# Seven products of quarters for eight in the first product of two squared-ReLU stages

## The chip, the cores and the metric

The kernel runs on one core of a Trainium2 chip, as one launch. The metric is the device time of that core in microseconds (us), the median of the runs. Engines are named as in the profile: PE (TensorE matmul), PEld (its weight loads), DVE (the vector engine), ACT (the scalar engine), POOL (GpSimd), SP (the engine that issues most DMAs).

## What is computed

Two transformer blocks for 16 meta tokens and 512 tokens of width 1024, all in float32. The second block has two layers, each an attention followed by a squared-ReLU stage, and these two stages are what the change touches:

```python
def sq_relu_mlp(x, w1, w2):
    h = jax.nn.relu(x @ w1)
    return (h * h) @ w2
...
        hn = rms_norm(h, attn_norm[i])
        if i < N_A:
            h = h + dsa_attention(hn, a_w_in[i], ...)
        else:
            ...
            h = h + fox_attention(hn, b_w_q[j], ...)
        h = h + sq_relu_mlp(rms_norm(h, mlp_norm[i]), mlp_w1[i], mlp_w2[i])
```

`w1` is 1024 x 4096 and `w2` 4096 x 1024. The first stage works on T = 528 tokens, the second on the S = 512 that are asked for.

## The kernel before

Activations are kept transposed: 8 tiles of 128 partitions (features) by the tokens. A float32 product is made of three float32r matmuls: each factor is split into a high part (a rounded copy, by ACT) and a low part (the difference, by DVE), and high x high, high x low and low x high are summed in PSUM. For weights this is `weight_parts` (`wh` at L82 by ACT, `wl` at L83 by DVE), for activations `split` (L106 and L107, or L109 and L110 where a factor per partition goes in).

`products` (matmul at L99) makes a block of 128 outputs: 8 tiles of depth x 3 matmuls for each stretch of tokens. In the first squared-ReLU stage a block takes two stretches of 264 tokens, in the second, where `k.whole` is set, one of 512. So a pair of blocks costs 2 x 2 x 24 = 96 matmuls of 264 columns there, and 2 x 24 = 48 of 512 columns here.

`mlp` (L1390) runs a stage. It first has the attention before it add its heads' outputs to the residual `h` (`before()`, which is `Dsa.out` at L1004 for the first stage and `Fox.out` at L1464 for the second): for each of 8 output tiles j a block of products from the attention's output (`bigh`, `bigl`), added to `h` by DVE (L857). `operand` (L893) then makes the stage's input from `h` times the norm's weights, split into `xh` and `xl` (L109, L110), one tile at a time, and sums the squares (ACT at L159 and L162, POOL at L163). `token_rsqrt` (L900) sums them over the partitions with 5 matmuls (L171), takes 1/sqrt by twelve small DVE operations (L131 to L138) and brings the result to all partitions with 5 transposes (L182) and two ACT copies (L907). These factors enter when the products are taken out of PSUM (L1407), so the products don't wait for them.

The 32 blocks of `w1` come in two chunks of 16. Each block is taken out by DVE (L1407, ReLU and norm), squared by ACT (L1410) and split (L106, L107). After a chunk `down` (L934, matmul at L948) multiplies its 16 tiles by `w2`, 8 output tiles at a time of two blocks of weights each, and DVE adds the result to `h` (L857). PSUM has 6 banks for products and 2 for the rest.

The order of the instructions on each engine is fixed when the program is built: a scheduler with a model of the engines' times puts them in order (the program's order gives the priority), and each engine then works its list strictly in order, waiting on semaphores. SP issues the weights' loads in its own list; a buffer of weights (`wr`, three of 512 KB) is free again when DVE has split it.

Of the kernel before, what the change touches and what calls it, by code (L numbers as in the profile page):

```python
# [46 lines left out]
class K:  # L47
    """The kernel's context: engines, pools and the pieces that recur."""

    def __init__(self, tc):  # L50
# [4 lines left out]

    def psum(self, **banks):
        """A pool of PSUM banks, so many a tag, for a phase."""
        self.banks = banks
# [14 lines left out]
    def weights(self, wdram, kt=8):  # L73
        """A block of kt tiles of weights, split into two float32r parts that sum to it exactly."""
# [11 lines left out]
    def dense(self, wdram, xh, xl, evac, kt=8, lo=0, n=T):  # L86
        """One block of 128 outputs for n tokens, a bank of them at a time: evac(products, tokens) takes them over."""
# [60 lines left out]
    def squares(self, tiles, pool=None, lo=0, eng=None):  # L148
        """Sums over the tiles of their squares from token lo on, [128, tokens] with zeros around."""
# [15 lines left out]
    def sumsq(self, acc, chunks):  # L165
        """The sums over the partitions too, as columns of PSUM (a column a chunk of tokens)."""
# [7 lines left out]
    def rows(self, cols, chunks, take, tags=("pa", "pa")):  # L174
        """The transposes of cols(chunk) [tokens, 128], to take(values, tokens)."""
# [44 lines left out]
# -------------------------------------------------------------------- first layer  # L220
# blocks of w_in: a head's q, k, v, then z, sc_b, sc_c, sc_x, gate_a, gate_b
# [9 lines left out]
class Layer1:  # L231
# [13 lines left out]
    def normed(self, out, lo=0):  # L245
        """Takes over the products of the tokens from lo on with their norm."""
# [47 lines left out]
    def gates(self):  # L294
        """Log decays, their running sums by chunks and betas."""
# [7 lines left out]
        with tc.tile_pool(name="l1g", bufs=1) as pg:  # L303
            G = self.G  # rows 0..15 beta, 32..47 decay; no decay where there is no token
# [118 lines left out]
    def sc_out(self, j):  # L423
        """2 sigmoid(gate_b) y_b for 128 features, in place of the gate."""
# [7 lines left out]
    # ---- independent of the recurrence  # L432
# [1422 lines left out]
```

## Time and profile before

| | |
|---|---|
| median of 3 runs | 2609.57 us (2607.39 to 2611.97) |
| span of the profiled execution | 2607.7 us, 1.9 us below that median; no separate time of this execution is listed |
| PE busy | 2523.1 us, 97% of the span |
| DVE, ACT, POOL busy | 1535.0, 1072.2, 438.4 us |
| mean granted TensorE clock | 0.979 of full speed |
| first squared-ReLU stage | about 1522 to 1895 us after the span's start |
| second squared-ReLU stage | about 2244 to 2604 us |

Matmuls overlap in the pipe, so PE's busy share says little about how close matmuls follow each other; the number of matmuls that start in a stretch of a window says it. The rows of a timeline give start, duration, engine, source line, what is written and read, and in brackets how long the engine had been idle and who released it.

### The profile page before, as it was taken

Reading aid. Unit: us, or ns where it says so; the run is one execution under the profiler, and the core shown is the slowest. Engines: PE = TensorE matmul, PEld = TensorE weight load, DVE = VectorE, ACT = ScalarE, POOL = GpSimd, SP = SyncE. Lnnn points to the kernel's source line nnn. Section 1 sums busy time; section 2 is a strip of 40 time slices with the busy share of each in tenths; the row PEclk is TensorE's granted clock in tenths of the full one; section 3 lists DMA queues with packets and bytes.
Section 4 is the critical chain, followed back from the end, with each engine's and each line's share of the span. In section 5 each row is a group of like instructions: output and inputs, shape, how many; then the busy total and the mean of one; then the engine's idle time right before and its main releaser. Section 6 shows DMA issues by size and latency. Waiting matters only on the chain.

```text
span 2607.7 us, 45619 instructions
## 1 busy us (share of the span) xinstructions
PE 2523.1 (97%) x18012; PEld 2315.5 (89%) x18012; DVE 1535.0 (59%) x3288; ACT 1072.2 (41%) x2191; POOL 438.4 (17%) x599
## 2 busy tenths in 40 slices
PE   8899999999999999999879999999999999999999
PEld 8889999999899888888868999999999988788887
DVE  7878788766554444335998454244555767642432
ACT  5434445353423322333546543133334766431331
POOL 2322212100002111013641010000112444100000
PEclk9999999999999999999978999999999989999999
DMA  4334333524552332333321232223333222232332
GB/s 152 94 95 121 84 96 90 118 89 133 169 204 89 97 97 92 96 90 109 87 71 39 62 114 90 90 89 95 119 95 97 83 72 65 90 95 91 97 105 81
DMA packets 139206, 257.20 MB, mean 99 GB/s; under 512 B 65536, under 2 KB 69664, under 8 KB 138992
## 3 DMA queue, kind: packets, MB, share of 16 engines
q1 hardware_dynamic: 82176, 236.46, 29.2%
q10 hardware_dynamic: 56816, 17.82, 3.5%
q8 instruction: 142, 2.33, 0.4%
q14 instruction: 72, 0.59, 0.1%
HBM read 223.39 MB, written 22.34 MB: 94 GB/s over the span
## 4 chain that ended last, share of the span: by engine, by line
PE 79%; DVE 11%; DMA 3%; ACT 2%; issue 1%; POOL 0%; ACTq 0%; SPq 0%; DVEq 0%; POOLq 0%
PE ps_pd L99 46%; PE ps_pd L948 19%; PE ps_pa L1349 2%; PE ps_po L1664 2%; PE ps_pb L662 1%; DVE prod L839 1%; DVE wl L83 1%; PE ps_pt L1653 1%; PE ps_pt L1339 1%; DVE sc L1280 1%; DVE sc L1268 1%; DMA Dn<-gsc 1%; DVE m L1279 1%; DVE t L1086 1%; DMA blk<-nd 1%
## 5 line engine op out<-in xcount | busy, mean ns | idle before, releaser
L82 ACT ACTIVATE wh<-wr 128x1024 fp32r<-128x1024 f32 (+2 forms) x367 | 379.4, 1034 | 966.7 <-PE ps_pd L99 470.1
L99 PE MATMUL ps_pd<-bigh,wh 128*128 128x256 f32 (+5 forms) x2256 | 695.5, 310 | 17.7 <-ACT bigh L109 6.5
L99 PE MATMUL ps_pd<-bigh,wl 128*128 128x256 f32 (+5 forms) x2256 | 692.5, 308 | 5.4 <-DVE wl L83 5.4
L99 PE MATMUL ps_pd<-bigl,wh 128*128 128x256 f32 (+5 forms) x2256 | 692.5, 308 | 1.2 <-DVE bigl L110 1.0
L83 DVE TENSOR_TENSOR wl<-wr,wh 128x1024 fp32r<-128x1024 f32 (+2 forms) x355 | 429.1, 1209 | 314.9 <-ACT wh L82 308.8
L99 PEld LDWEIGHTS ps_pd<-bigh,wh 128*128 128x128 f32 (+1 forms) x2256 | 430.8, 191 | 39.5 <-ACT bigh L109 6.7
L99 PEld LDWEIGHTS ps_pd<-bigh,wl 128*128 128x128 f32 (+1 forms) x2256 | 430.9, 191 | 24.0 <-DVE wl L83 6.8
L99 PEld LDWEIGHTS ps_pd<-bigl,wh 128*128 128x128 f32 (+1 forms) x2256 | 431.0, 191 | 20.4 <-DVE bigl L110 3.0
L99 PE MATMUL ps_pd<-xh,wh 128*128 128x264 f32 (+1 forms) x1040 | 327.4, 315 | 1.2 <-ACT t L1544 1.2
L99 PE MATMUL ps_pd<-xh,wl 128*128 128x264 f32 (+1 forms) x1040 | 326.4, 314 | 0.8 <-DVE wl L83 0.8
L99 PE MATMUL ps_pd<-xl,wh 128*128 128x264 f32 (+1 forms) x1040 | 325.8, 314 | 0.0
L948 PE MATMUL ps_pd<-fh,wh 128*128 128x264 f32 (+1 forms) x944 | 315.6, 334 | 0.0
L948 PE MATMUL ps_pd<-fh,wl 128*128 128x264 f32 (+1 forms) x944 | 315.6, 334 | 0.0
L948 PE MATMUL ps_pd<-fl,wh 128*128 128x264 f32 (+1 forms) x944 | 315.4, 334 | 0.0
L99 PEld LDWEIGHTS ps_pd<-xh,wh 128*128 128x128 f32 x1040 | 196.7, 189 | 13.8 <-ACT t L1544 2.1
L99 PEld LDWEIGHTS ps_pd<-xh,wl 128*128 128x128 f32 x1040 | 196.8, 189 | 12.7 <-DVE wl L83 1.3
L99 PEld LDWEIGHTS ps_pd<-xl,wh 128*128 128x128 f32 x1040 | 196.9, 189 | 11.7
L948 PEld LDWEIGHTS ps_pd<-fh,wl 128*128 128x128 f32 x944 | 177.2, 188 | 19.5
L948 PEld LDWEIGHTS ps_pd<-fh,wh 128*128 128x128 f32 x944 | 177.2, 188 | 19.5
L948 PEld LDWEIGHTS ps_pd<-fl,wh 128*128 128x128 f32 x944 | 177.3, 188 | 19.3
L163 POOL TENSOR_TENSOR acc<-acc,sq 128x512 f32<-128x512 f32 (+1 forms) x35 | 62.1, 1773 | 602.7 <-ACT sq L162 592.8
L857 DVE TENSOR_TENSOR h<-ps_pd,h 128x256 f32<-128x256 f32 (+3 forms) x112 | 56.2, 502 | 163.9 <-PE ps_pd L948 129.3
(448 smaller groups left out, 3944.2 us busy)
## 6 DMA issues: line engine op xcount, KB each, us to landing
wr<-wm SPq DMA_DIRECT2D x128, 512.0 KB
wr<-w SPq DMA_DIRECT2D x72, 512.0 KB
wr<-wgu SPq DMA_DIRECT2D x44, 512.0 KB
wr<-wa SPq DMA_DIRECT2D x17, 512.0 KB
wr<-wkv SPq DMA_DIRECT2D x17, 512.0 KB
wr<-wdn SPq DMA_DIRECT2D x16, 512.0 KB
wr<-wao SPq DMA_DIRECT2D x16, 512.0 KB
ck<-cd SPq DMA_DIRECT2D x16, 264.0 KB
```

The source lines that it names most:

```text
L82: nc.scalar.activation(wh, wr, AF.Copy)
L83: (self.low or nc.vector).tensor_tensor(wl, wr, wh, ALU.subtract)
L99: nc.tensor.matmul(ps[:, :half], a[:, k], b[k][:, ts], start=(k == 0 and i == 0), stop=(k == kt - 1 and i == 2))
L163: (eng or nc.vector).tensor_tensor(acc, acc, sq, ALU.add)
L662: nc.tensor.matmul(pq[r, c, :w], lhs(pr)[:, c], rhs(pr)[:, c], start=True, stop=True)
L839: nc.vector.tensor_tensor(prod[:, :i, :i], X[:, :i, :i], bt[:, :i, i].rearrange("p (o j) -> p o j", o=1).broadcast_to([2 * H, i, i]), ALU.mult
L857: k.nc.vector.tensor_add(v, ps, v)
L948: nc.tensor.matmul(pss[h][:, :half], a[:, q], b[f0 + q][:, ts], start=(f0 + q == 0 and i == 0), stop=(f0 + q == nf - 1 and i == 2),)
L1086: nc.vector.tensor_tensor(t, t, sw, ALU.add)
L1268: nc.vector.scalar_tensor_tensor(acc[:n, c0:c1], rl[:n, : c1 - c0], wi[:n, i, hd : hd + 1], acc[:n, c0:c1], ALU.mult, ALU.add)
L1349: nc.tensor.matmul(O[b][:, g], pT[:m, c], self.V[:m, c, 64 * g : 64 * g + 64], start=(c == 0), stop=(c == nch - 1))
L1664: nc.tensor.matmul(po, V[: ns[c], c, par].rearrange("p a n -> p (a n)"), t[: ns[c], c - g], start=(c == 0 and t is hi), stop=(c == nch - 1 ...
```

## The change

In both squared-ReLU stages the first product is made by Strassen's method in Winograd's form. A pair of output blocks (256 outputs) is cut into quarters: depth in halves of 512, outputs in halves of 128, tokens in halves of 264 (256 in the second stage). Seven products of quarters take the place of eight.

- `seven` makes the products of a pair: 7 x 4 x 3 = 84 matmuls of 264 (256) columns. It needs the four quarters of the weights, and four sums of them; the first two sums are made by DVE, the other two by POOL, then all seven are split as before (`part`: ACT and DVE, three of 1024 columns and one of 512). Two products add to a bank that was read out before. Loads come as four of 256 KB per pair, into three buffers of the old pool and two of a new one (`wq`).
- `Squares` combines the products: DVE adds five times per pair, ACT copies once and takes the ReLU and the square.
- `combined` takes the place of `operand`: 7 operands of 4 quarter tiles, each split, with sums and differences between. Their tiles lie in `xh`, `xl` and in `bigh`, `bigl`, which the attention's outputs occupy until `before()` has used them. The squares for the norm follow behind it.
- The factor of the norm is no longer applied before the square: its square is applied when the second product is taken out, by an operation of DVE of its own (`add`). There are 4 chunks of 8 blocks and not 2 of 16, so that `down` takes out twice as often.
- All 8 banks of PSUM are for products and share their ring with the rest. `before` makes its tiles in the order 0, 4, 1, 5, 2, 6, 3, 7.

The other hunks remove comments. Core of the diff:

```diff
     def pst(self, tag="pa"):
+        tag = tag if tag in self.banks else "pd"
...
+    def seven(self, wdram, x, n, evac):
...
+        pools = (self.wp, self.wq, self.wp, self.wq)
+        g1, g2, g3, g4 = (p.tile([128, 2, 512], F32, name="wr", tag="wr", bufs=self.wr_bufs - (p is self.wq)) for p in pools)
+        wd = wdram.rearrange("p q k m -> p q (k m)")
+        nc.sync.dma_start(g2[:, 1], wd[:, 3])
+        nc.sync.dma_start(g4[:, 0], wd[:, 1])
+        nc.sync.dma_start(g1[:, 0], wd[:, 0])
+        nc.sync.dma_start(g3[:, 0], wd[:, 2])
+        nc.vector.tensor_tensor(g2[:, 0], g2[:, 1], g1[:, 0], ALU.add)
+        nc.vector.tensor_tensor(g2[:, 1], g2[:, 1], g4[:, 0], ALU.add)
+        nc.gpsimd.tensor_tensor(g1[:, 1], g2[:, 0], g4[:, 0], ALU.add)
+        nc.gpsimd.tensor_tensor(g3[:, 1], g1[:, 1], g3[:, 0], ALU.add)
...
+        def part(i, g, m):
+            wh, wl = (pools[i].tile([128, 8, 128], F32R, name=x, tag=x, bufs=self.ws_bufs) for x in ("wh", "wl"))
+            v = g[:, :m].rearrange("p q (k m) -> p (q k) m", m=128)
+            nc.scalar.activation(wh[:, : 4 * m], v, AF.Copy)
+            nc.vector.tensor_tensor(wl[:, : 4 * m], v, wh[:, : 4 * m], ALU.subtract)
...
+        x1, u, y, v = bank(), bank(), bank(), bank()
+        a11, s2 = part(0, g1, 2)
+        product(x1, a11, "b11")
+        evac.first(x1)
+        product(u, s2, "t2")
+        evac.second(u)
+        s3, s1 = part(1, g2, 2)
+        product(y, s3, "t3")
+        product(v, s1, "t1")
+        evac.third(v)
+        a12, s4 = part(2, g3, 2)
+        product(x1, a12, "b21", start=False)
+        evac.out11(x1)
+        evac.out22(y)
+        z = bank()
+        product(z, s4, "b22")
+        evac.out12(z)
+        (a22,) = part(3, g4, 1)
+        product(y, a22, "t4", start=False)
+        evac.out21(y)
...
+class Squares:
...
+    def second(self, ps):
+        self.nc.vector.tensor_tensor(self.u2, ps, self.p1, ALU.add)
...
+    def out21(self, ps):
+        self.nc.vector.tensor_tensor(self.u[:, 1, : self.half], ps, self.u2, ALU.add)
+        v = self.u[:, 1, : self.n]
+        self.nc.scalar.activation(v, v, AF.Relu, scale=-1.0)
+        self.done(1)
+    def done(self, i):
+        v = self.u[:, i, : self.n]
+        self.nc.scalar.activation(v, v, AF.Square)
+        self.k.split(self.outs[i][0][:, : self.n], self.outs[i][1][:, : self.n], v)
...
+def combined(k, h, x, norm, lo, n, pool):
...
+    for i in range(4):
+        p, q = k.par(norm, i), k.par(norm, i + 4)
+        put("b11", i, h[:, i, a], p)
+        put("b21", i, h[:, i + 4, a], q)
+        g22 = pool.tile([128, T // 2], F32, name="g22", tag="fh", bufs=RING)[:, :m]
+        nc.scalar.activation(g22, h[:, i + 4, b], AF.Copy, scale=q)
+        put("b22", i, g22)
+        g12 = pool.tile([128, T // 2], F32, name="g12", tag="fh", bufs=RING)[:, :m]
+        nc.scalar.activation(g12, h[:, i, b], AF.Copy, scale=p)
+        t = pool.tile([128, T // 2], F32, name="gt", tag="fl", bufs=RING)[:, :m]
+        nc.vector.tensor_tensor(t, g22, g12, ALU.subtract)
+        put("t3", i, t)
...
+        nc.vector.scalar_tensor_tensor(t, h[:, i, a], p, g12, ALU.mult, ALU.subtract)
+        put("t1", i, t)
+        nc.vector.tensor_tensor(g22, g22, t, ALU.add)
+        put("t2", i, g22, -1.0)
+        nc.vector.scalar_tensor_tensor(t, h[:, i + 4, a], q, g22, ALU.mult, ALU.subtract)
+        put("t4", i, t, -1.0)
...
 def mlp(k, io, h, i, before, lo=0, n=T):
...
-        before()
-        acc = operand(k, h, xh, xl, f"mnorm{i}", lo)
+        before((0, 4, 1, 5, 2, 6, 3, 7))
...
+        combined(k, h, x, f"mnorm{i}", lo, n, s)
+        acc = k.squares(tiles(h), lo=lo, eng=nc.gpsimd)
         rs = token_rsqrt(k, p, acc)
+        nc.vector.tensor_tensor(rs, rs, rs, ALU.mult)
...
+                nc.vector.tensor_tensor(y, ps, rs[:, t], ALU.mult)
+                nc.vector.tensor_add(h[:, j, t], h[:, j, t], y)
...
+        for c in range(CHUNKS):
+            f = [[s.tile([128, T], F32R, name=x_, bufs=RING) for x_ in ("fh", "fl")] for _ in range(part)]
+            for j in range(0, part, 2):
+                k.seven(w1[(i * nf + c * part + j) // 2], x, n, Squares(k, s, n, f[j : j + 2]))
+            down(k, w2[8 * i : 8 * i + 8, :, c * part : c * part + part], *zip(*f), part, add, n=n)
+CHUNKS = 4
...
-RING = 19
+RING = 10
```

The order of instructions changes with it. PE, where the first squared-ReLU stage starts. L99 is the matmul of `products` (with `bigh`, `bigl` still the attention's output, with `xh`, `xl` the stage's own product); L171 sums the squares, L182 transposes the norm's factors. Before:

```order
L99 MATMUL ps_pd<-bigl,wh 128x272
L99 MATMUL ps_pd<-bigh,wl 128x272
L99 MATMUL ps_pd<-xh,wh 128x264
L99 MATMUL ps_pd<-xl,wh 128x264
...
L171 MATMUL ps_pa<-ones_69,acc 128x1 x5
L99 MATMUL ps_pd<-xh,wh 128x264
...
L182 MATMUL ps_pa<-idn,rcol 128x128 x4
L182 MATMUL ps_pa<-idn,rcol 128x16
L99 MATMUL ps_pd<-xh,wl 128x264
```

And now (L100 is the matmul of `products`, L234 and L245 are the former L171 and L182, L136 is the matmul of `seven`):

```order
L100 MATMUL ps_pd<-bigl,wh 128x272
L100 MATMUL ps_pd<-bigh,wl 128x272
L234 MATMUL ps_pd<-ones_69,acc 128x1 x5
L245 MATMUL ps_pd<-idn,rcol 128x128 x4
L245 MATMUL ps_pd<-idn,rcol 128x16
L136 MATMUL ps_pd<-xh,wh 128x264
L136 MATMUL ps_pd<-xl,wh 128x264
L136 MATMUL ps_pd<-xh,wl 128x264
```

Before, 51 of the stage's own matmuls stood ahead of the sums and 53 more ahead of the transposes; now none does. The second stage's start has the same order, with 72 matmuls of `before` ahead of it (in the order before, 35 more stood ahead of the sums).

DVE, the same place, the last operand work and what follows (`bigl` and `xl` are low parts of the seven operands, `gt` and `g` their sums and differences; L194 to L201 are the twelve steps of 1/sqrt, L1465 is the first sum of products):

```order
L1506 SCALAR_TENSOR_TENSOR bigl<-gt,bigh 128x264 x2
L1525 SCALAR_TENSOR_TENSOR gt<-h,params,g_16728 128x264
L1506 SCALAR_TENSOR_TENSOR bigl<-g_16728,bigh 128x264
L1506 SCALAR_TENSOR_TENSOR bigl<-gt,bigh 128x264
L194 TENSOR_SCALAR rsv<-ps_pd 128x5
L195 TENSOR_SCALAR rst<-rsv 128x5
...
L201 SCALAR_TENSOR_TENSOR rcol<-rsa,rcol 128x5
L1552 TENSOR_TENSOR rrow<-rrow 128x528
L1465 TENSOR_TENSOR u_16823<-ps_pd,p_16822 128x264
```

From the first L920 (the former L857, adding the attention's output to `h`) to the last L201 stand 78 operations: 8 of L920, 6 splits of the attention's weights (L84), 44 of `combined` with 264 columns, 4 sums of weights of 512 columns (L119, L120), 4 splits of the pair's weights (L129: 3 of 1024 columns, 1 of 512) and the 12 steps. In the second stage they are the same 78, with 512 columns for L920, 384 for L84 and 256 for the 44.

## Rows read from the trace of the kernel before

**Rows 1.** The profile's page: busy us (share of the span) and instructions.

```profile
PE 2523.1 (97%) x18012; PEld 2315.5 (89%) x18012; DVE 1535.0 (59%) x3288; ACT 1072.2 (41%) x2191; POOL 438.4 (17%) x599
```

**Rows 2.** Windows: stretch, length, busy (instructions) by engine, PE clock, DMA share, GB/s.

```profile
750.00:800.00 50.00, 50.00 (x423) 50.00 (x422) 28.63 (x47) 16.30 (x21) 3.37 (x2) 1.00 0.41 135
...
1650.00:1700.00 50.00, 50.00 (x412) 50.00 (x411) 13.70 (x17) 9.50 (x9) 0.00 (x0) 1.00 0.30 94
...
2400.00:2450.00 50.00, 50.00 (x217) 40.45 (x217) 17.80 (x20) 14.18 (x17) 0.00 (x0) 1.00 0.30 95
```

**Rows 3.** Timeline of PE and DVE around the start of the first stage.

```profile
1500.82 0.44 DVE L857 TENSOR_TENSOR h<-ps_pd,h 128x272 f32<-128x272 f32 x1 [5.78 <-PE ps_pd L99]
...
1507.89 1.23 DVE L83 TENSOR_TENSOR wl<-wr,wh 128x1024 fp32r<-128x1024 f32 x1 [0.58 <-ACT wh L82]
1509.03 0.76 DVE L110 SCALAR_TENSOR_TENSOR xl<-h,params,xh 128x528 fp32r<-128x528 f32 x1
...
1521.80 0.29 PE L99 MATMUL ps_pd<-xh,wh 128*128 128x264 f32 x1
...
1530.23 0.16 DVE L131 TENSOR_SCALAR rsv<-ps_pa 128x5 f32<-128x5 f32 x1
...
1532.43 0.17 DVE L138 SCALAR_TENSOR_TENSOR rcol<-rsa,rcol 128x5 f32<-128x5 f32 x1
...
1535.54 0.75 PE L182 MATMUL ps_pa<-idn,rcol 128*128 128x128 f32 x5
1536.87 1.44 DVE L1407 SCALAR_TENSOR_TENSOR u<-ps_pd,rrow 128x264 f32<-128x264 f32 x4
```

**Rows 4.** Timeline of PE, DVE and POOL around the start of the second stage.

```profile
2210.90 0.42 DVE L107 TENSOR_TENSOR bigl<-o,bigh 128x256 fp32r<-128x256 f32 x1
2211.28 0.42 DVE L1674 TENSOR_TENSOR o<-ps_po,ow 64x256 f32<-64x256 f32 x1
...
2229.50 0.69 DVE L857 TENSOR_TENSOR h<-ps_pd,h 128x512 f32<-128x512 f32 x1 [3.94 <-PE ps_pd L99]
...
2231.18 0.55 DVE L83 TENSOR_TENSOR wl<-wr,wh 128x384 fp32r<-128x384 f32 x1
2231.64 1.41 DVE L110 SCALAR_TENSOR_TENSOR xl<-h,params,xh 128x512 fp32r<-128x512 f32 x2
...
2235.08 1.30 POOL L163 TENSOR_TENSOR acc<-acc,sq 128x512 f32<-128x512 f32 x1 [0.87 <-ACT sq L162]
2235.15 1.77 DVE L110 SCALAR_TENSOR_TENSOR xl<-h,params,xh 128x512 fp32r<-128x512 f32 x1
...
2238.99 0.74 DVE L110 SCALAR_TENSOR_TENSOR xl<-h,params,xh 128x512 fp32r<-128x512 f32 x1
...
2244.44 0.39 PE L99 MATMUL ps_pd<-xh,wh 128*128 128x512 f32 x1
```

**Rows 5.** Groups by form, 2229 to 2250 us, DVE (count, busy, mean ns, idle before).

```profile
L110 DVE SCALAR_TENSOR_TENSOR xl<-h,params,xh 128x512 fp32r<-128x512 f32 x8 | 9.2, 1156 | 0.0
L857 DVE TENSOR_TENSOR h<-ps_pd,h 128x512 f32<-128x512 f32 x8 | 5.5, 683 | 4.1 <-PE ps_pd L99 3.9
L83 DVE TENSOR_TENSOR wl<-wr,wh 128x384 fp32r<-128x384 f32 x6 | 5.4, 894 | 0.0
```

**Rows 6.** Groups by form, 1500 to 1525 us, DVE and POOL.

```profile
L163 POOL TENSOR_TENSOR acc<-acc,sq 128x528 f32<-128x528 f32 x7 | 12.9, 1838 | 52.0 <-ACT sq L162 52.0
...
L110 DVE SCALAR_TENSOR_TENSOR xl<-h,params,xh 128x528 fp32r<-128x528 f32 x8 | 6.1, 762 | 0.0
```

**Rows 7.** Windows before and after the clock rises ahead of the first stage.

```profile
1495.00:1500.00 5.00, 4.91 (x21) 4.91 (x22) 0.04 (x1) 0.00 (x0) 0.00 (x0) 0.50 0.00 0
1500.00:1525.00 25.00, 25.00 (x199) 25.00 (x199) 18.77 (x24) 17.77 (x24) 11.76 (x7) 0.99 0.49 148
```

**Rows 8.** Groups by form, 1560 to 1630 us, DVE's and ACT's splits.

```profile
L107 DVE TENSOR_TENSOR fl<-u,fh 128x528 fp32r<-128x528 f32 x11 | 7.8, 709 | 0.0
...
L82 ACT ACTIVATE wh<-wr 128x1024 fp32r<-128x1024 f32 x12 | 12.7, 1061 | 44.0 <-PE ps_pd L99 35.6 <-PE ps_pd L948 8.4
```

More of the change, by code (lines that the diff above doesn't have):

```diff
@@ L100, in products, with product, bank @@
             evac(ps[:, :half], slice(h * half, (h + 1) * half))
+    def seven(self, wdram, x, n, evac):
+        nc = self.nc
+        half = n // 2
+        pools = (self.wp, self.wq, self.wp, self.wq)
[9 more added lines that the diff above has]
+        nc.gpsimd.tensor_tensor(g3[:, 1], g1[:, 1], g3[:, 0], ALU.add)
+        parts = {}
+        def part(i, g, m):
[3 more added lines that the diff above has]
+            nc.vector.tensor_tensor(wl[:, : 4 * m], v, wh[:, : 4 * m], ALU.subtract)
+            return [(wh[:, 4 * i : 4 * i + 4], wl[:, 4 * i : 4 * i + 4]) for i in range(m)]
+        def product(ps, w, b, start=True):
+            (wh, wl), (bh, bl) = w, x[b]
+            for q in range(4):
+                for i, (a, c) in enumerate(((wh, bh), (wh, bl), (wl, bh))):
+                    nc.tensor.matmul(
+                        ps, a[:, q], c[:, q], start=(start and q == 0 and i == 0), stop=(q == 3 and i == 2),
+                        skip_group_check=not start,
+                    )
+        def bank():
+            return self.pst("pd")[:, :half]
+        x1, u, y, v = bank(), bank(), bank(), bank()
[18 more added lines that the diff above has]
+        evac.out21(y)
@@ L1002, in run, with out @@
             self.attend()
-    def out(self, early=False, js=range(8)):
+    def out(self, js=range(8), early=False):
         k = self.k
@@ L1373, in attend @@
                 k.low = nc.gpsimd if DLOW else None
[L1374 removed]
+                self.out((DOUT.index(i),), True)
                 k.low = None
@@ L1386, with __init__, first, third @@
 DOUT = tuple(range(40, 56, 2))
+class Squares:
+    def __init__(self, k, s, n, outs):
+        self.k, self.nc, self.s, self.n, self.half, self.outs = k, k.nc, s, n, n // 2, outs
+        self.u = s.tile([128, 2, T], F32, name="u", bufs=2)
+        self.p1, self.u2, self.w = (s.tile([128, T // 2], F32, name=x, bufs=2)[:, : self.half] for x in ("p1", "u2", "w"))
+    def first(self, ps):
+        self.nc.scalar.activation(self.p1, ps, AF.Copy)
+    def second(self, ps):
+        self.nc.vector.tensor_tensor(self.u2, ps, self.p1, ALU.add)
+    def third(self, ps):
+        self.nc.vector.tensor_tensor(self.w, ps, self.u2, ALU.add)
+    def out11(self, ps):
+        self.nc.scalar.activation(self.u[:, 0, : self.half], ps, AF.Relu)
+    def out22(self, ps):
+        self.nc.vector.tensor_tensor(self.u[:, 1, self.half : self.n], ps, self.w, ALU.add)
+    def out12(self, ps):
+        v = self.u[:, 0, self.half : self.n]
+        self.nc.vector.tensor_tensor(v, ps, self.w, ALU.add)
+        self.nc.scalar.activation(v, v, AF.Relu)
+        self.done(0)
+    def out21(self, ps):
[7 more added lines that the diff above has]
+        self.k.split(self.outs[i][0][:, : self.n], self.outs[i][1][:, : self.n], v)
@@ new lines, in combined, with put @@
+def combined(k, h, x, norm, lo, n, pool):
+    nc = k.nc
+    m = n // 2
+    a, b = slice(lo, lo + m), slice(lo + m, lo + n)
+    def put(name, i, v, scale=None):
+        hi, lw = (t[:, i, :m] for t in x[name])
+        if scale is None:
+            k.split(hi, lw, v)
+        else:
+            nc.scalar.activation(hi, v, AF.Copy, scale=scale)
+            nc.vector.scalar_tensor_tensor(lw, v, scale, hi, ALU.mult, ALU.subtract)
+    for i in range(4):
[10 more added lines that the diff above has]
+        put("t3", i, t)
+        t = pool.tile([128, T // 2], F32, name="gt", tag="fl", bufs=RING)[:, :m]
+        nc.vector.scalar_tensor_tensor(t, h[:, i, a], p, g12, ALU.mult, ALU.subtract)
[4 more added lines that the diff above has]
+        put("t4", i, t, -1.0)
@@ L1462, in part, with out @@
             k.dense(self.io["wbo"][j][:, a:b], oh[a:b], ol[a:b], residual(k, self.h, NM)(j), kt=b - a, n=S)
-    def out(self):
-        self.part(FPART, 8)
+    def out(self, js):
+        self.part(FPART, 8, js)
     def queries(self):
@@ L1823, in layout @@
     o["wao"] = blocks(wo.reshape(D, D))
-    o["wm1"] = np.concatenate([blocks(w) for w in mlp_w1_2])
+    o["wm1"] = np.concatenate([quarters(blocks(w)) for w in mlp_w1_2])
     o["wm2"] = np.concatenate([blocks(w) for w in mlp_w2_2])
```

39 lines of the change are left out of this document (24 added, 15 removed).

## The prediction

> **What bounds the kernel now.** First the page: PE is busy for 97% of the span, DVE for 59%, ACT for 41% [rows 1]. What the reader should see is that time goes only where fewer matmuls follow each other, or where PE waits. Then the windows, by the number of matmuls that start in 50 us [rows 2]. In the first squared-ReLU stage 412 of 264 columns start, one each 121.4 ns, with no gap and the clock at its full 2.4 GHz; in the second 217 of 512 columns, one each 230.4 ns. Matmuls of 256 columns, which the second stage has after the change, can be seen elsewhere in the program: 423 in 50 us, one each 118.2 ns. So inside both stages PE alone sets the time: DVE is busy for 14 to 18 of the 50 us. Last the timelines at the two places where the stages start [rows 3, 4], since there PE has to be fed with operands that don't exist yet. Before the change PE goes over without a stop: its first own matmul follows the attention's last at 1521.80 and at 2244.44, because the operands were made tile by tile in the shadow of the attention's products.
>
> **What is saved.** There are 16 pairs of blocks in each stage. First stage: 96 - 84 = 12 matmuls a pair less, 16 x 12 x 121.4 ns = 23.3 us. Second stage: 48 x 230.4 = 11.06 us a pair become 84 x 118.2 = 9.93 us, 16 x 1.13 = 18.1 us. Together **41.4 us** less on PE. The order shows 336 matmuls of `seven` in each chunk of 4 pairs, so the count itself is sure. Loads move the same bytes, and the second product has the same matmuls.
>
> **What the starts of the stages cost.** In the new order the five sums of squares and the five transposes stand on PE ahead of every matmul of `seven`, and on DVE the 12 steps of 1/sqrt that the transposes wait for stand behind all 44 operations of `combined`. So the stage's first matmul can't start before DVE has worked off all 78 operations, whatever is ready. Behind that wait stands PE's whole list. The factor of the norm is needed only at the end of the chunk; it is its place in the lists that costs.
>
> The price of one, as the distance to the next: 1.14 us for a split of 1024 columns, 0.44 for adding 272 columns of PSUM, 0.20 for one of the 12 steps (11 distances from 1530.23 to 1532.43) [rows 3], 0.38 for 256 columns of two SBUF tensors and 0.46 for 384 [rows 4], 0.69 at most for 512 [rows 5].
>
> First stage: 8 x 0.44 + (6 + 3) x 1.14 + 44 x 0.38 + 5 x 0.69 + 12 x 0.20 = 3.5 + 10.3 + 16.7 + 3.4 + 2.4 = 36.3 us from the first addition at 1500.82 [rows 3]. Second stage: 8 x 0.69 + 6 x 0.46 + 3 x 1.14 + 16.7 + 3.4 + 2.4 = 34.2 us from 2229.50 [rows 4]. In the shadow of the attention's products (21 and 15 us) there was room for about half of it.
>
> To this comes what GpSimd takes from DVE. In the second stage's start seven POOL additions run beside DVE, and splits that take 0.74 and 0.55 us alone take 1.156 and 0.894 on average [rows 4, 5]: 8 x 0.42 + 6 x 0.34 = 5.4 us, 0.77 for each POOL addition. The single case shows how: the split at 2235.15 takes 1.77, because it gets through only after the POOL addition of 2235.08 to 2236.38 has ended [rows 4]. Additions to `h`, which read PSUM and only one SBUF tensor, keep their 0.68 [rows 5]. Ahead of the first stage the same seven POOL additions cost DVE nothing (762 ns a split) and were themselves slow (1838 ns) [rows 6]: DVE had pauses there. So an addition on POOL costs DVE between 0 and 1.3 us. I take 0.77, since DVE's list after the change has no pauses at these places, as in rows 5. Before the transposes stand up to 11 POOL additions in the first stage (7 of squares, 4 of weights) and 9 in the second.
>
> [...]
>
> So the first matmul of `seven` starts at 1500.82 + 36.3 + 8.5 + 0.75 for the five transposes [rows 3] = 1546.4 in the first stage, 24.6 us after 1521.80; without any delay by POOL at 1537.9 (16.1), with 1.3 each at 1552.2 (30.4). In the second at 2229.50 + 34.2 + 6.9 + 0.75 = 2271.4, 26.9 us after 2244.44; bounds 20.0 and 31.7. Together **51.5 us** (36.1 to 62.1). Here ACT is not the one that is late: it has about as many operations, but each split needs ACT first, so a part of its time adds to DVE's; that stays in the upper bound.
>
> After such a pause PE starts at the lower clock. Ahead of the first stage, after pauses of DVE's and ACT's making, the granted clock was 0.50 (1.2 GHz) for a stretch of 5 us in which 21 matmuls started; at full clock it is 199 in 25 us, 40 in 5 [rows 7]. So a stretch of that length costs 19 x 126 ns = 2.4 us. Two such starts are new: **4.8 us** (0 to 5.2).
>
> **Inside the stages.** A pair takes PE 84 x 121.4 = 10.2 us in the first stage and 9.9 in the second. DVE has per pair 3 splits of 1.14, three operations of 512 columns of 0.69, five sums out of PSUM of 0.36 (four in 1.44) and two splits of 0.71 [rows 3, 5, 8]: 3.4 + 2.1 + 1.8 + 1.4 = 8.7 us, and 2 POOL additions x 0.77 = 1.5, together 10.2. That is PE's own time. ACT with three copies of 1.06 [rows 8] and eight smaller ones stays under it. Relief comes from `down`, in which DVE has 1.14 + 2 x 0.8 us per 5.8 us of PE: there the first pair of the next chunk is prepared. So three of four pairs are tight, and what is late then is the next split of weights. Bounds: nothing, and with 1.3 per POOL addition 11.3 - 10.0 = 1.3 us for each of 24 pairs, 30 us. I take **4 us**, near the lower end, since at 0.77 the sums are equal. The ends of the chunks (8 for 4) should cost nothing: behind the last product stand 47 matmuls of `down`, 5.7 us, before the first that needs the last tile, whose sum, ReLU, square and split take some 3 us. The extra operation of `add` is hidden but for the very last, 0.7 us. The loads are as many bytes in smaller pieces and run ahead; the rest of the program keeps its lists but for small exchanges.
>
> **Sum.** -41.4 + 51.5 + 4.8 + 4 + 0.7 = +19.6 us. Against the profiled span of 2607.7 that is 2627.3; the median of the runs lies 1.9 us above that span, so 2629.
>
> **Rivals.**
> - *The starts are cheap.* DVE and POOL pass each other freely, as in rows 6, the 44 operations follow at 0.36 as those out of PSUM (1.8 us less over both stages), the clock stays up and nothing is lost inside. Then -41.4 + 36.1 - 1.8 + 0.7 = -6.4: 2603 us, faster than before. For it: DVE was idle for 6 of the 25 us ahead of the first stage [rows 7]. Against it: rows 5. It decides if the first matmul of `seven` starts before about 1537 and 2263.
> - *The pairs are bound by DVE and POOL.* Each POOL addition blocks DVE for its whole 1.3 us, in every tight pair: 30 us in place of 4, 2655 us. For it: the split of 1.77 us; against it: sums out of PSUM don't need the shared path. It decides from 0.9 us per POOL addition on.
> - That the change doesn't do what it says is excluded by the counts of matmuls in the order.
>
> **How the numbers follow.** Forecast 0.62, first rival 0.17, second 0.17, something unseen in the reordered rest 0.04. The range leaves out the outermost of both rivals: from 2605 to 2655. A measurement of this kernel can tell some 0.2%, 5.2 us, from no change. Faster by more: half of the first rival and a little of the unseen, 0.11. Within it: the rest of the first rival and the forecast's lower end, where POOL costs DVE next to nothing, 0.13. Slower: 0.76.
>
> **What would show it.** Right: in the profile after, two pauses of PE of 20 to 30 us, each ended by the matmul L234 or L245 on work of DVE, a window with clock 0.50 behind each, and splits of 264 columns that take 0.44 alone and over 1 us beside POOL; inside the stages 412 and 423 matmuls in 50 us. Wrong: the first L136 within 16 us of the attention's last product, or less than 400 matmuls in 50 us in the middle of a chunk.

## The result, and the profile after

The change makes the kernel **slower by 1.3%**: 2648.03 us (median of 4 runs, 2644.37 to 2650.40) against 2610.77 us for the kernel before in the same comparison; the ratio is 1.0134, with a 95% interval from 1.0113 to 1.0154. The profiled execution took 2644.37 us, its span is 2642.7 us, 35.0 more than the 2607.7 of before.

Both traces can be cut at the same five events: the first addition of the attention's output to `h` (DVE, L857 before, L920 now) and the first own product of `xh`, in each stage, and between them the first product of `bigl` in the attention that follows the first stage (0.2 us behind that attention's very first matmul in both).

| stretch, us | before | after | difference | forecast |
|---|---|---|---|---|
| to the first addition of the first stage | 1500.8 | 1505.8 | +5.0 | 0 |
| from there to the stage's first own product | 21.0 | 49.0 | +28.0 | +24.6 |
| from there to the next attention's first product of `bigl` | 376.6 | 357.0 | -19.6 | -18.9 |
| that attention, to the second stage's first addition | 331.1 | 333.5 | +2.5 | 0 |
| from there to the stage's first own product | 14.9 | 45.0 | +30.1 | +26.9 |
| from there to the end | 363.3 | 352.3 | -11.0 | -13.0 |
| sum | 2607.7 | 2642.7 | +35.0 | +19.6 |

So the stages' own time grew by 27.5 us (58.1 at the starts, -30.6 behind them), and 7.5 us came from stretches that the change doesn't touch. (The forecast's -18.9 is -23.3 + 2.4 + 2, its -13.0 is -18.1 + 2.4 + 2 + 0.7.)

The profile's page of the changed kernel answers to [rows 1]:

```profile
PE 2494.5 (94%) x18396; PEld 2313.8 (88%) x18396; DVE 1771.6 (67%) x3698; ACT 1191.5 (45%) x2439; POOL 550.7 (21%) x663
```

Windows of the changed kernel (stretch, length, busy and instructions by engine, PE clock, DMA share, GB/s) answer to [rows 2]: first the inside of the first stage, then the first stage's start in pieces of 5 us, with 15 us of products of the second stage between.

```profile
1600.00:1650.00 50.00, 50.00 (x412) 50.00 (x411) 31.48 (x51) 13.69 (x16) 6.21 (x4) 1.00 0.24 76
...
2296.00:2311.00 15.00, 15.00 (x130) 15.00 (x129) 11.15 (x17) 9.12 (x14) 3.77 (x2) 1.00 0.22 72
...
1525.00:1530.00 5.00, 3.04 (x22) 2.81 (x22) 5.00 (x7) 4.02 (x8) 1.90 (x1) 1.00 0.17 52
1530.00:1535.00 5.00, 0.00 (x0) 0.00 (x0) 5.00 (x8) 5.00 (x13) 4.27 (x2) 0.62 0.42 137
1535.00:1540.00 5.00, 0.00 (x0) 0.00 (x0) 5.00 (x8) 2.01 (x5) 2.30 (x2) 0.50 0.21 70
...
1550.00:1555.00 5.00, 1.43 (x6) 1.07 (x7) 2.99 (x15) 0.92 (x3) 0.00 (x0) 0.50 0.00 0
1555.00:1560.00 5.00, 5.00 (x29) 5.00 (x30) 0.94 (x2) 0.99 (x3) 0.00 (x0) 0.65 0.00 0
1560.00:1565.00 5.00, 5.00 (x44) 5.00 (x43) 3.52 (x5) 2.14 (x3) 0.00 (x0) 1.00 0.17 52
```

Inside the stages the matmuls follow each other as before, 412 of 264 columns in 50 us. At the start PE does nothing for ten us in a row while DVE is busy for 5.00 of every 5. (A window counts every instruction that reaches into it, so 130 in 15 us are some 127 starts, one each 118 ns.) PE's timeline there, first of the first stage, then of the second, answers to [rows 3, 4] (in brackets how long PE had stood and who ended it; a row with x5 or x10 merges several matmuls):

```profile
1525.81 0.39 PE L100 MATMUL ps_pd<-bigh,wl 128*128 128x272 f32 x1 [1.61 <-DVE wl L84]
1544.75 2.29 PE L234 MATMUL ps_pd<-ones,acc 128*128 128x1 f32 x10 [15.91 <-POOL acc L226]
1553.57 1.33 PE L245 MATMUL ps_pd<-idn,rcol 128*128 128x128 f32 x5 [6.52 <-DVE rcol L201]
1554.83 0.59 PE L136 MATMUL ps_pd<-xh,wh 128*128 128x264 f32 x1
...
2262.46 0.80 PE L100 MATMUL ps_pd<-bigh,wl 128*128 128x512 f32 x1 [3.90 <-DVE wl L84]
2275.82 2.29 PE L234 MATMUL ps_pd<-ones,acc 128*128 128x1 f32 x10 [10.01 <-POOL acc L226]
2289.11 1.33 PE L245 MATMUL ps_pd<-idn,rcol 128*128 128x128 f32 x5 [11.00 <-DVE rcol L201]
2290.36 0.58 PE L136 MATMUL ps_pd<-xh,wh 128*128 128x256 f32 x1
```

In both starts the first pause ends with POOL's last addition of the squares, the second with DVE's last step of 1/sqrt. DVE's list is what sets the start: from its first L920 to its last L201 (47.7 and 43.7 us) DVE itself stands still for 1.5 us in the first stage and 0.2 in the second, so neither ACT nor a load holds it up for long, and when PE has summed the squares it still has 6.5 and 10.9 us of work ahead of the transposes. Why that list takes so long stands in the timeline of DVE and POOL in the first stage's start:

```profile
1538.86 0.42 DVE L170 TENSOR_TENSOR bigl<-gt,bigh 128x264 fp32r<-128x264 f32 x1
1539.02 1.38 POOL L121 TENSOR_TENSOR wr<-wr 128x512 f32<-128x512 f32 x1 [2.45 <-DVE wr L119]
1539.20 1.49 DVE L1506 SCALAR_TENSOR_TENSOR bigl<-g,bigh 128x264 fp32r<-128x264 f32 x1
1540.37 1.48 POOL L226 TENSOR_TENSOR acc<-acc,sq 128x528 f32<-128x528 f32 x1
1540.62 1.52 DVE L170 TENSOR_TENSOR bigl<-gt,bigh 128x264 fp32r<-128x264 f32 x1
1541.81 1.45 POOL L122 TENSOR_TENSOR wr<-wr 128x512 f32<-128x512 f32 x1
1542.06 1.48 DVE L1506 SCALAR_TENSOR_TENSOR xl<-h,params,xh 128x264 fp32r<-128x264 f32 x1
1543.22 1.48 POOL L226 TENSOR_TENSOR acc<-acc,sq 128x528 f32<-128x528 f32 x1
1543.47 1.52 DVE L1525 SCALAR_TENSOR_TENSOR gt<-h,params,g 128x264 f32<-128x264 f32 x1
1544.91 0.42 DVE L1518 TENSOR_TENSOR gt<-g,g 128x264 f32<-128x264 f32 x1
```

In these rows a split that takes 0.42 to 0.48 us takes 1.5 when an addition of POOL runs beside it, and each ends some 0.3 us behind that addition: POOL and DVE take turns. DVE isn't always the one that waits: from 1520.69 us on three of its operations with two SBUF tensors kept their 0.42 and 0.68 us, and POOL's addition beside them took 2.54. The first stage's start has 11 operations of DVE that were held up in this way, by 11.2 us together (each one's duration less that of the same form alone), for 11 POOL additions; the second has 11.5 us, also for 11.

### The profile page after: what moved, and what is told of

The parts are those of the page before. It is cut to its first block, busy times and chain, and to the rows that moved or that the text cites. A ratio compares the mean times of both kernels' runs of the same rounds, so it can differ in the third digit from the quotient of the medians.

```text
span 2642.7 us, 47487 instructions
## 1 busy us (share of the span) xinstructions
PE 2494.5 (94%) x18396; PEld 2313.8 (88%) x18396; DVE 1771.6 (67%) x3698; ACT 1191.5 (45%) x2439; POOL 550.7 (21%) x663
## 5 line engine op out<-in xcount | busy, mean ns | idle before, releaser
L100 PE MATMUL ps_pd<-bigh,wh 128*128 128x256 f32 (+5 forms) x2256 | 695.6, 310 | 17.6 <-ACT bigh L172 6.3
L100 PE MATMUL ps_pd<-bigh,wl 128*128 128x256 f32 (+5 forms) x2256 | 693.8, 309 | 10.5 <-DVE wl L84 10.5
L100 PE MATMUL ps_pd<-bigl,wh 128*128 128x256 f32 (+5 forms) x2256 | 692.5, 308 | 1.0 <-DVE bigl L173 0.8
L83 ACT ACTIVATE wh<-wr 128x1024 fp32r<-128x1024 f32 (+3 forms) x303 | 311.1, 1028 | 658.5 <-PE ps_pd L100 266.3
L100 PEld LDWEIGHTS ps_pd<-bigh,wh 128*128 128x128 f32 (+1 forms) x2256 | 431.0, 191 | 39.6 <-ACT bigh L172 6.3
L100 PEld LDWEIGHTS ps_pd<-bigh,wl 128*128 128x128 f32 (+1 forms) x2256 | 430.5, 191 | 30.1 <-DVE wl L84 12.8
L84 DVE TENSOR_TENSOR wl<-wr,wh 128x1024 fp32r<-128x1024 f32 (+3 forms) x291 | 350.0, 1203 | 152.3 <-ACT wh L83 144.6
L100 PEld LDWEIGHTS ps_pd<-bigl,wh 128*128 128x128 f32 (+1 forms) x2256 | 430.7, 191 | 20.1 <-DVE bigl L173 2.0
L128 ACT ACTIVATE wh<-wr 128x1024 fp32r<-128x1024 f32 (+1 forms) x128 | 119.9, 950 | 154.6 <-PE ps_pd L1011 55.7
L129 DVE TENSOR_TENSOR wl<-wr,wh 128x1024 fp32r<-128x1024 f32 (+1 forms) x128 | 160.7, 1269 | 15.9 <-ACT wh L128 14.8
L121 POOL TENSOR_TENSOR wr<-wr 128x512 f32<-128x512 f32 x32 | 51.8, 1618 | 451.8 <-DMA wr<-wm 192.8
L136 PE MATMUL ps_pd<-xl,wh 128*128 128x264 f32 (+1 forms) x512 | 145.4, 285 | 0.0
L136 PE MATMUL ps_pd<-xh,wh 128*128 128x264 f32 (+1 forms) x512 | 145.0, 285 | 0.0
L136 PE MATMUL ps_pd<-xh,wl 128*128 128x264 f32 (+1 forms) x512 | 144.9, 285 | 0.0
L1558 DVE TENSOR_TENSOR y<-ps_pd,rrow 128x264 f32<-128x264 f32 (+1 forms) x96 | 49.1, 516 | 101.9 <-PE ps_pd L1011 101.7
```

Source lines behind the costliest of these rows:

```text
L83: nc.scalar.activation(wh, wr, AF.Copy)
L84: (self.low or nc.vector).tensor_tensor(wl, wr, wh, ALU.subtract)
L100: nc.tensor.matmul(ps[:, :half], a[:, k], b[k][:, ts], start=(k == 0 and i == 0), stop=(k == kt - 1 and i == 2))
L121: nc.gpsimd.tensor_tensor(g1[:, 1], g2[:, 0], g4[:, 0], ALU.add)
L128: nc.scalar.activation(wh[:, : 4 * m], v, AF.Copy)
L129: nc.vector.tensor_tensor(wl[:, : 4 * m], v, wh[:, : 4 * m], ALU.subtract)
```

## The experiments

The stages' times below are cut as in the table above: from the first addition to the next attention, and to the end. Before: 397.6 and 378.2 us; changed: 406.0 and 397.3.

**Fewer additions on GpSimd (no_squares).** The additions of the squares are left out.

```diff
-            (eng or nc.vector).tensor_tensor(acc, acc, sq, ALU.add)
+            if eng is None or not self.skip:
+                (eng or nc.vector).tensor_tensor(acc, acc, sq, ALU.add)
```

> Edit: the changed kernel without the seven GpSimd additions that sum the squares in each of the two stages (the norm's factor is taken from the first tile alone). Theory F with the price read from the changed kernel's starts (11 operations of DVE with some 1.0 us too much in each): seven additions less are 7 us less for each start: 2632 to 2636 us. Rival (DVE would have waited for ACT or for the next tile in that time, the standstills are covered): 1 to 2 us for each start, 2644 to 2648 us.

Measured: 2626.53 us, ratio to before 1.0048 (1.0029 to 1.0066). The first product comes 40.9 and 36.3 us after the first addition in place of 49.0 and 45.0: 8.1 and 8.8 us earlier for seven additions, 1.2 us for each. That is somewhat above the 1.0 of the trace, and the rival falls. The total lies 5.5 us below the expected range; in the profiles 5.6 us less is spent outside the stages than with the change (below). What stays, in the list of PE's waits in the first start (who waited for whom: us in total, times, the longest), is a single wait for DVE (L247 is L245 there, L202 is L201):

```profile
PE ps_pd L247 <- DVE rcol L202: 17.4, 1, 17.4
```

**The same additions on DVE (sums_dve).** L121, L122 and the squares' additions by `nc.vector` in place of `nc.gpsimd`.

> Edit: GpSimd's additions for the two stages, those of the weights' sums (L121, L122) and those of the squares, are made by DVE; the order of the program is as in the changed kernel. Theory A (an operation of DVE with two SBUF operands stands still until a GpSimd addition beside it has ended): an addition costs DVE some 1.0 us when GpSimd makes it (11 operations of DVE that took 1.4 to 2.3 us in the first stage's start in place of 0.4 to 1.2) and 0.69 when DVE makes it itself. Each start gets shorter by 11 x 0.3 = 3.5 us, and the pairs inside have 0.6 us less: faster than the changed kernel by 7 to 14 us, 2634 to 2641 us. Rival D (DVE is bound by the number of its own operations, what GpSimd makes is free): 22 more operations of 0.69 us in the two starts, +15 us, and two more in each tight pair, up to 1.4 us for each of 24: 2663 to 2695 us.

Measured: 2651.52 us, 1.0145 (1.0129 to 1.0161). The starts got shorter by 2.1 and 3.9 us (46.9 and 41.1): an addition costs DVE less when it makes it itself, as theory A says, and not 0.69 us more, as D says. But the rest of the stages got longer, 359.6 and 358.0 us for 357.0 and 352.3. There PE's waits behind L1474 (the sum that must be out of a bank before the next product adds to it) are 9.4 us in the second stage, where the changed kernel has 4.1:

```profile
PE ps_pd L136 <- DVE u L1474: 9.4, 7, 2.1
```

So theory A holds for the starts and not for the total, which lies 10 us above its range and below D's.

**Fewer operands (no_sums).**

```diff
-        t = pool.tile([128, T // 2], F32, name="gt", tag="fl", bufs=RING)[:, :m]
...
-        put("t4", i, t, -1.0)
+        for a, b in (("t3", "b22"), ("t1", "b11"), ("t2", "b21"), ("t4", "b22")):
+            x[a] = x[b]
```

> Edit: the changed kernel without t1 to t4; the products that use them read b11, b21 and b22 in their place. This leaves out 28 operations of DVE and 16 of ACT in each start (the sums of the activations and their splits). Theory F (a start lasts as long as DVE's whole list there, wherever the norm stands): 28 operations of 0.34 to 0.40 us are 10 us less for each start, so the first product comes some 10 us earlier in both stages: 2626 to 2630 us. Rival (the chain over ACT, or GpSimd's additions, sets the start): less than 5 us for each, 2638 us or more.

Measured: 2628.67 us, 1.0057 (1.0035 to 1.0079). The first product comes 42.2 and 35.9 us after the first addition, 6.8 and 9.1 us earlier. The total is in theory F's range and the starts are nearer to it than to the rival, but both gain less than its 10 us, and the list of PE's waits shows that here the rival has a part:

```profile
PE ps_pd L234 <- POOL acc L226: 12.7, 1, 12.7
```

Without the sums DVE has worked off its list 4.9 and 4.8 us before it can take the squares' sums from PE, which waits for POOL's last addition. So DVE's list sets the starts of the changed kernel, but the chain over POOL stands close behind it. The two edits took 16.9 and 15.9 us off the starts, each in a kernel of its own; were they to add up, that would be 32.8 of the 58.1 us that the starts grew by. The rest was not taken apart.

**The norm moved away (norm_late).**

```diff
-        acc = k.squares(tiles(h), lo=lo, eng=nc.gpsimd)
-        rs = token_rsqrt(k, p, acc)
-        nc.vector.tensor_tensor(rs, rs, rs, ALU.mult)
...
                 k.seven(w1[(i * nf + c * part + j) // 2], x, n, Squares(k, s, n, f[j : j + 2]))
+            if c == 0:
+                acc = k.squares(tiles(h), lo=lo, eng=nc.gpsimd)
+                rs = token_rsqrt(k, p, acc)
+                nc.vector.tensor_tensor(rs, rs, rs, ALU.mult)
```

> Edit: the squares for the norm, their sums and the twelve steps of 1/sqrt with the transposes are written behind the first chunk's products and ahead of its down, in both stages; nothing else is changed. Theory A (it is the place of the norm in the lists that costs): PE's first L136 no longer waits for the 12 steps (2.4 us), the transposes and the copies (some 1.5), and the squares' seven GpSimd additions no longer stop DVE during a start (about 1 us each in the changed kernel's trace). That is 11 us for each start, 22 together, of which some comes back inside the first chunk: 2626 to 2633 us. Rival B (the seven operands themselves are late): the last low part of t2 stands only two to five operations of DVE ahead of the 12 steps, and the second product needs it, so PE stops again after its first 12 matmuls; only the steps and the transposes go away, the additions of the squares are met again inside: about 2643 us.

Measured: 2647.46 us, 1.0133 (1.0113 to 1.0154), no different from the change itself; the stages take 406.6 and 396.4 us. PE's first L136 comes after 22.8 and 19.4 us in place of 49.0 and 45.0, and yet nothing is won. PE's waits from 1506 to 1600 us show it: one long wait has become many short ones, for the operands (L1506, L169), the weights (L129, L128) and at last the norm, 18 us in all, and between them PE runs slowly (windows from 1525 us).

```profile
PE ps_pd L136 <- DVE xl L1506: 4.2, 2, 3.4
PE ps_pd L245 <- DVE rcol L201: 4.0, 1, 4.0
PE ps_pd L136 <- DVE wl L129: 3.0, 3, 1.3
PE ps_pd L136 <- ACT wh L128: 2.7, 1, 2.7
```

```profile
1525.00:1550.00 25.00, 17.14 (x93) 15.23 (x94) 25.00 (x37) 14.90 (x31) 13.00 (x8) 0.78 0.16 52
1550.00:1575.00 25.00, 20.98 (x159) 20.41 (x158) 17.94 (x28) 14.55 (x25) 5.38 (x3) 0.94 0.30 90
```

Theory A falls, and B's 5 us aren't there either. Moving the norm alone wins nothing, since the operands and the weights are late too.

**The chunks alone, in the kernel before (chunks4).** `half = nf // 4`, `range(4)`, `RING = 10`.

> Edit in the kernel before: the outputs of the first product come in 4 chunks of 8 blocks and not 2 of 16 (rings of 10 buffers and not 19); the products stay the eight of before, the norm is applied where it was. The forecast took nothing for the ends of the chunks: 2608 to 2613 us. Rival E (each new end of a chunk stops PE for one to two us, as the windows with 37 to 42 matmuls of 512 columns in 10 us at the ends of the changed kernel's second stage suggest): 4 more ends, 2615 to 2619 us.

Measured: 2613.17 us, 1.0001 (0.9990 to 1.0012); stages of 398.3 and 378.1. The ends of chunks cost nothing in the kernel before; rival E falls there.

**Plain products while DVE makes the sums (plain2, plain4, plain3).** `eight` makes a pair by 2 x 2 blocks of 24 matmuls from the quarters, without sums.

```diff
+        for c, names in enumerate((("b11", "b21"), ("b12", "b22"))):
+            for o, (wh, wl) in enumerate(w):
+                ps = self.pst("pd")[:, :half]
...
+                evac.plain(ps, o, c)
...
+                if c == 0 and j == 2:
+                    sums()
+                (k.eight if c == 0 and j < 4 else k.seven)(w1[(i * nf + c * part + j) // 2], x, n, q)
```

> Edit: in each stage the first two pairs are made by the eight plain products of quarters (which need b12 split in place of the sums), the sums t1 to t4 are written behind the first of these pairs, and the norm stands behind the first chunk's products. Theory A (the cost is only that the seven operands must exist before the first product): four pairs give back 12 matmuls each, 2 x 12 x 121.4 + 2 x 12 x 118.2 ns = 5.7 us, and the two starts, some 58 us with 5 us of the lower clock behind them, nearly vanish, since PE has 23 us of plain products while DVE makes the sums: about 2592 us, from 2585 to 2600, faster than the kernel before. Rival C (the load of DVE and GpSimd is only moved, and the third pair waits for it): half of the starts' cost comes back as stops after the second pair: about 2620 us.

Measured: 2620.46 us, 1.0030 (1.0018 to 1.0043); stages of 393.3 and 385.9. The first product now comes after 19.6 and 17.1 us, and still rival C is right. PE's waits, a row of DVE's timeline and the windows in the first stage's start show where it went:

```profile
PE ps_pd L274 <- DVE rcol L230: 3.5, 1, 3.5
PE ps_pd L187 <- DVE bigl L199: 2.3, 3, 1.1
```

```profile
1531.92 4.42 DVE L199 TENSOR_TENSOR bigl<-g,bigh 128x264 fp32r<-128x264 f32 x3
```

```profile
1530.00:1535.00 5.00, 3.08 (x24) 2.66 (x22) 5.00 (x4) 2.00 (x5) 4.92 (x4) 0.97 0.15 52
1535.00:1540.00 5.00, 4.14 (x16) 3.52 (x17) 3.48 (x4) 1.04 (x3) 2.42 (x2) 0.50 0.00 0
1540.00:1545.00 5.00, 5.00 (x37) 5.00 (x37) 1.00 (x1) 2.12 (x4) 0.00 (x0) 0.84 0.01 3
```

The low parts of b12 come late (three splits of 264 columns take 4.42 us), since POOL is busy for 4.92 of 5 us with squares and weights that nobody needs yet. Four stops of PE of 0.4 to 1.1 us follow, and from the second of them on the granted clock is at 0.50 (1.2 GHz): in the window from 1535 us 16 matmuls are counted and not 41, partly for the stops in it and partly for the clock. The norm's transposes (L274) stop PE once more ahead of `down`. Hence the next two: a longer plain part, and the norm in three steps.

> Edit: as with two plain pairs, but all four pairs of the first chunk are made by the eight plain products; the squares are written behind the second pair, the 1/sqrt behind the fourth, and the transposes only where the first result of down needs them. Against the kernel before, 12 pairs save 12 x 1.46 us in the first stage and 12 x 1.13 in the second, four pairs cost 0.3 each in the second: 17.5 + 13.6 - 1.2 = 30 us. Theory F (the work of the starts is hidden if PE has plain products for as long as DVE needs): what is lost are the stops for b12 with the low clock behind them, 5 to 10 us: 2585 to 2593 us. Rival C (short stops, each with a stretch of low clock, take the saving back, as with two plain pairs): 2600 to 2612 us.

> Edit: as with four plain pairs, but three. Theory F: one more pair saves 1.5 + 1.4 us, if the fourth pair's operands and weights are ready in time: 2583 to 2592 us. If DVE is not done by then, a stop and a low clock at the fourth pair in each stage, 3 to 5 us each: 2592 to 2600 us.

Measured: with four plain pairs 2604.08 us, 0.9962 (0.9947 to 0.9977), stages of 383.9 and 371.5; with three **2597.19 us, 0.9936 (0.9916 to 0.9956)**, stages of 382.0 and 371.8. Both are faster than the kernel before. The stages are shorter by 20.4 and 22.0 us, for four pairs what theory F gives (30 less 5 to 10). The totals are 11 and 5 us above theory F's ranges and lie in those of the rivals; the stages' times speak for F, and the rest lies outside the stages (below). Against two plain pairs both the number of pairs and the place of the norm were changed, and what each of them gives was not separated. PE's waits with three pairs in the first start are down to short ones:

```profile
PE ps_pd L187 <- DVE bigl L199: 1.4, 1, 1.4
PE ps_pd L100 <- DVE wl L84: 1.3, 1, 1.3
PE ps_pd L100 <- ACT wh L83: 1.1, 1, 1.1
```

**All weight sums on GpSimd (plain3_pool).** Inside the stages the changed kernel stops PE at seven places, for 5.5 us together, at the matmul behind L1474, each time in the last pair of a chunk. Its timeline of DVE and PE at one of them:

```profile
2490.59 0.69 DVE L170 TENSOR_TENSOR fl<-u,fh 128x512 fp32r<-128x512 f32 x1
2493.14 0.69 DVE L120 TENSOR_TENSOR wr<-wr 128x512 f32<-128x512 f32 x1 [1.85 <-DMA wr<-wm]
2493.75 0.42 DVE L1468 TENSOR_TENSOR w<-ps_pd,u 128x256 f32<-128x256 f32 x1
2494.20 0.42 DVE L1474 TENSOR_TENSOR u<-ps_pd,w 128x256 f32<-128x256 f32 x1
...
2494.68 0.39 PE L136 MATMUL ps_pd<-bigh,wh 128*128 128x256 f32 x1 [1.11 <-DVE u L1474]
```

DVE isn't too busy there: it stands for 1.85 us in front of L120, whose load hasn't landed, and the sums that PE needs are behind it in DVE's list. At the other six it stands there for 1.26 to 1.85 us.

> Edit: the kernel with three plain pairs, and all four sums of a pair's weights are made by GpSimd (L119 and L120 too, which DVE made). Theory G (inside the stages PE stops because DVE, working its list in order, stands in front of L120 until a load has landed, with the sums of products that PE needs behind it): the stops at the matmul behind L1474, 4.4 us in both stages with three plain pairs, go away, and DVE has 1.4 us less per pair, against some 1 us for each of two GpSimd additions more: 2592 to 2596 us, faster than with three plain pairs by 1 to 5. Rival (GpSimd's four additions in a row, 1.3 to 1.9 us each and DVE stopped beside them, come too late for the splits of the weights): 2600 us or more.

Measured: 2611.16 us, 0.9999 (0.9989 to 1.0009); stages of 387.1 and 376.2, 5.1 and 4.4 longer than with three plain pairs. The waits behind that sum are indeed gone, but PE waits for the weights instead, as the rival says; in the second stage:

```profile
PE ps_pd L136 <- ACT wh L128: 6.3, 3, 2.5
```

**The time outside the stages (before_quarters, before_again, after_again).** Span less both stages is 1831.9 us before and 1839.4 after; in the first eight kernels made from the change, itself included, it lies between 1833.8 and 1845.8. In `before_quarters` the loads of L82's blocks read the layout of the change.

> Edit in the kernel before: w1 of both stages lies in memory by quarters, as in the change, and a block comes by two loads of 256 KB in place of one of 512; nothing else. In the eight profiles of kernels made from the change the first addition of the first stage's start comes at 1502.9 to 1507.4 us, in the two made from the kernel before at 1499.7 and 1500.8, though the lists are the same up to there. Theory H (it has to do with the layout or the smaller loads): 1504 us or later, 2616 us or more. Rival (it has not): 1499 to 1502 us and 2609 to 2614 us.

> The kernel before, unchanged, profiled once more. In its first profile the time outside the two stages is 1831.9 us and the first addition of the first stage's start comes at 1500.8 us; with w1 by quarters it was 1839.3 and 1506.1. Theory N (a single execution varies by several us ahead of the stages, whatever the program): another value than the first, anywhere from 1500 to 1507 us. Rival P (each program has its own time there): within 1 us of 1500.8.

> The changed kernel, unchanged, profiled once more. In its first profile the two stages take 406.0 and 397.3 us, the rest 1839.4, and the first addition comes at 1505.8 us. Theory N: the stages within 1 us of these values, since they are set by DVE's list and PE's; the rest anywhere from 1832 to 1847 us. Rival P: both within 1 us.

Measured: w1 by quarters 2613.11 us, 1.0002 (0.9990 to 1.0015), though its one profile has the first addition at 1506.1 us and 1839.3 us outside the stages; the kernel before once more 2608.95 us, 0.9990 (0.9974 to 1.0005), with 1829.0 us outside; the changed kernel 2645.83 us, 1.0138 (1.0096 to 1.0181), stages of 407.9 and 398.1, and 1839.0 us outside. The second profile of the changed kernel has its first addition at 1504.4 us, and its first stage is 1.9 us longer than in the first profile, more than either theory allowed. So a single profile varies by some us (N): the profile by quarters is that of the slowest of its ten runs, and its time outside the stages is that of the changed kernel, though its median is that of the kernel before. What can be said for a difference of the programs rests on the medians: the change costs 37.3 us in the first comparison and 34.5 in the last (two runs), of which the stages of the profiles hold 27.5 and 30.2, so some 4 to 10 us are left outside. The layout of w1 and the number of chunks, whose ratios are 1, don't bring them by themselves. In the profile after, DVE's same operations come 0.5 us later than in the one before at 100 us and 5.8 us later at 700 us, and that stays so up to 1200 us: the delay arises far ahead of the stages. In the profile with w1 by quarters it is 5.9 us at 700 us. Its cause stays open.

## Why the prediction was right in direction and short in size

- **PE's saving** (41.4 us): right. The page counts 384 matmuls more, 84 + 84 in place of 96 + 48 for each of 16 pairs, and the rates are in the windows: 412 matmuls in 50 us in the first stage, 130 in 15 us in the second.
- **The starts** (51.5 us forecast, 58.1 measured): the mechanism was right, PE waits for DVE's whole list; the term was mis-sized, by 3.4 and 3.2 us. The step that failed is "I take 0.77": a POOL addition costs DVE 1.0 us by the trace of the change (11.2 and 11.5 us for 11) and 1.2 by the run without seven of them. And in the second stage 11 of them stood ahead, not 9. With 11.2 and 11.5 us the terms of 8.5 and 6.9 grow by 7.3 together; the miss is 6.6. That additions from PSUM keep their time was right too: L920 took 0.43 us at 1531.49 beside POOL, and from 1500 us on all 31 sums of 264 columns out of PSUM that met a POOL addition took 0.42 to 0.43. The Trainium skill's Advanced Engine Details and Errata (GPSIMD Details) and GPSIMD Engine Reference (Specifications) name vector instructions with two SBUF inputs among those that conflict with GpSimd, and there the trace agrees: 1.48 to 1.56 us for 0.42 to 0.48. The expected pauses of 20 to 30 us came in two parts at each start, 15.9 and 6.5 us, and 10.0 and 11.0; the first part was ended by POOL and not by DVE.
- **"It is its place in the lists that costs"**, said of the norm: wrong. With the norm moved behind the first chunk the time was the same (1.0133). The operands and the weights are late too, so its place only decided on which matmul PE stood.
- **The low clock** (4.8 us): about twice too much. The window with 0.65 has 29 matmuls where 41 would start, 12 x 0.12 = 1.5 us, and behind the second start (below) there are 34 where 42 would, 8 x 0.12 = 1.0 us. Ahead of the second start the last 512-column products follow each other at 0.43 us in place of 0.23, from 2262.46 on, but PE then stands for 10 us, so that costs nothing.

```profile
2290.00:2295.00 5.00, 5.00 (x34) 4.82 (x33) 1.14 (x2) 1.78 (x4) 0.00 (x0) 0.76 0.02 3
```

- **Inside the stages** (4 us, up to 30): near the lower end, as said, but 8 us. PE's waits there are 1.4 us in the first stage, and 4.1 behind L1474 and 2.5 at the starts of `down` in the second. Wrong in the reason: the stops behind L1474 come from DVE standing in front of a load, in the last pair of a chunk, not from DVE and POOL being full in three of four. "The loads ... run ahead" was too kind for the same reason. That the ends of the chunks cost nothing held in the kernel before (chunks4); in the changed kernel the 2.5 us at the starts of `down` stand there.
- **The sum of the stages**: 7.9 us short (27.5 for 19.6). The starts make 6.6 of it. The clock (2.3 less than forecast) and the stops inside (4 more) go against each other, so that the stretches behind the starts came out within 1.3 us (-30.6 for -31.9) is in part luck.
- **What was not in the sum**: 7.5 us outside the stages in this profile (4 to 10 by the medians), taken as nothing; its cause is open.
- **The rivals.** Cheap starts: refuted, since the first L136 came at 1554.8 and 2290.4 us. Pairs bound by DVE and POOL: its price per addition was right, above 0.9 us, but PE paid it only in the starts; its stops inside came to 8 us and not 30.

## What to carry to other kernels

A product that needs fewer matmuls needs its operands before the first of them; price the vector engine's whole list ahead of that first matmul, at the place where PE has nothing else to do, before counting matmuls. If there is plain work of the same stage, do that first: three plain pairs of sixteen in each stage, with the norm spread out behind them, turned a loss of 1.3% into a gain of 0.6% here. Moving one late item down the list wins nothing while the others are late too, and an addition given to GpSimd isn't free for a DVE that works on two SBUF tensors.

## What the runs showed of the hardware

In the changed kernel from 1500 us on, a DVE operation with two SBUF tensors that was held up by a GpSimd addition ended 0.3 us behind it with 256 or 264 columns (1.48 to 1.56 us for 0.42 to 0.48), 0.55 with 512 and 1.08 with 1024. Others kept their time, and the GpSimd addition took longer (2.54 us at 1520.69). DVE's sums out of PSUM kept theirs in every case there.

In the kernel with two plain pairs the granted clock fell to 0.50 at 1534.7 us, amid stops of PE of 1.1 and 0.8 us, and rose again at 1541.6. In the one with three, a single stop of 1.4 us in the same place left it at 1.00. In the changed kernel's first start it was at 0.50 from 1531.2 to 1558.5 us, the last 3.7 us of it with products running.

Profiles of programs whose lists for DVE agree over the first 1500 us reach the first addition of the first stage between 1499.7 and 1511.2 us; what decides it no run here shows.
